# Mixing steps after every sixth projection matmul, and attention in a written order on TensorE and SyncE

## The chip, the core and the metric

The kernel runs on one core of a Trainium2 chip. The metric is the device time of one execution in microseconds (us). TensorE multiplies matrices into PSUM; VectorE, ScalarE and GpSimd work on what comes out; SyncE issues most DMAs. A difference of 0.2% (6 us) is about what a measurement of this kernel can tell from none.

## What is computed

One decoder block on 2048 tokens of width 1024, in float32. Its input projection feeds two groups of heads side by side: eight heads of RWKV-7 time mixing and four heads of differential attention. Output projection, a residual sum and a gated feed-forward part with a short convolution follow. Cut to what the change touches:

```
xn   = rms_norm(x);  proj = xn @ w_in            # 26 column blocks of 128
# time mixing, per token and head:
sa    = state @ (-kk)
state = state * w + sa (kk * a)^T + v k^T
y     = state @ r
# attention, per head h and query block of 128:
s_c  = q_c k_c^T / 8 - slope * distance, causal, c = 0, 1
attn = softmax(s_0) - lam * softmax(s_1)
o    = attn @ v
h    = x + rms_norm(concat(y_rwkv, o) @ w_out);  out = h + feed_forward(h)
```

## The kernel before

**Order of work.** Four stages follow each other: the projection with time mixing woven in, attention, the output projection, the feed-forward part. A planner orders each engine's instructions by readiness in its own time line and by source order. Inside `tc.manual_schedule(engines=...)` the instructions of the named engines keep the order of the source. Before, that holds for TensorE in the projection stage alone.

**Projection.** `Proj.product` makes one block of 128 columns by 512 tokens: 24 matmuls, three for each of eight k (high and low parts of the split operands, L293 to L295). After each three, `Pace.tick` runs every step that is due at that tick. The block is evicted by `shift` (for time mixing) or `evict` (for attention's Q, K, V) and goes to DRAM.

**Time mixing.** `Rwkv.group` is a generator for 128 tokens; there are 16, started `PITCH` = 34 ticks apart, so three are under way at once. Each `yield` names the tick at which the next step is due. The steps with matmuls, in order: z and za (L498, L500), n2 (L515), the turn of its result (L464), the spread (L470), bo (L550), two score steps (L563), V's turn (L582), two turns of keys (L592), wp (L607); then the join of two half inverses, which starts at `JOIN`: xp (L641), a product with bda (L647), one with bdx (L651); then for each of two chunks rp (L666), sp (L672), yp and up (L680 to L688); then mp, vs, a turn, a spread and gp. Between the scores and the join, VectorE runs a chain of 31 pairs of small operations (L612, L614) on data that goes through DRAM (adr, ab), and the result goes through DRAM too (xdr, x1t).

**Attention.** `Attn.steps` walks over 64 units, a head h and a query block qb of 128. `scores` makes, for both maps c, tiles of up to 512 keys in PSUM (L844, L845, and the causal mask L847 on the last); VectorE evicts each with its minimum (L849), ScalarE takes the exponentials (L858), VectorE combines the two maps (L869). `output`, for the unit two back (`LAG` = 2), transposes the weights in blocks of up to four (tp, L887), ScalarE copies them (at, L889), and the value products follow (op, L893). PSUM has four banks for scores, two for transposes, two for outputs. `fetch_k` loads 512 keys and values, `load_q` 256 queries, both from SyncE. After unit 6 `OutFfn.weights` loads w_out and the convolution's tables, splits w_out, and turns the tables on TensorE.

Of the kernel before, what the change touches and what calls it, by code (L numbers as in the profile page):

```python
# [18 lines left out]
P = 128  # L19
# [110 lines left out]
class Pace:  # L130
# [17 lines left out]

    def tick(self):
        self.run(self.now)  # L150
        self.now += 1

# [5 lines left out]
class Proj:  # L158
# [51 lines left out]
    def start(self, first):  # L210

        xs = [self.alloc(0, g) for g in range(2)]
        xt = []
        for t in range(HALF // P):
            if t == W0:
                self.weights(0, 0)
            if t == TB:
                tab = self.tables()
                self.weights(0, 1)
            xt.append(self.norm(t, first))  # L220
            if t < 4:
                for hf in range(2):
                    self.rows(t, hf, xt[t], xs[0])

        def rest():
            for i in range(8):
                t, hf = 4 + i // 2, i % 2
                self.rows(t, hf, xt[t], xs[1])
                yield 1 + 2 * i
        self.pace.add(tab, 6)  # L230
        self.pace.add(rest(), 1)
        for g in range(2):
            for cb in range(2):
                self.product(0, cb, g)
# [51 lines left out]
    def product(self, half, cb, g):  # L286
        nc, cx = self.nc, self.cx
        wh, wl = self.w[half, cb]
        xh, xl = self.x[half, g]
        n = f"{half}_{cb}_{g}"  # L290
        pp = cx.ps.tile([P, GRP], F32, name=f"pp{n}", tag=cx.mm[0], bufs=cx.mm[1])
        for k in range(KB):
            nc.tensor.matmul(pp, wh[:, k, :], xh[:, k, :], start=(k == 0), stop=False)  # L293
            nc.tensor.matmul(pp, wh[:, k, :], xl[:, k, :], start=False, stop=False)  # L294
            nc.tensor.matmul(pp, wl[:, k, :], xh[:, k, :], start=False, stop=(k == KB - 1))  # L295
            if k == KB - 1:
                self.evict(half, cb, g, pp, n)
            self.pace.tick()

# [50 lines left out]
ARB = 3  # L350
PITCH, JOIN = 34, 64
NGRP = S // RG
# [87 lines left out]
class Rwkv:  # L440
# [31 lines left out]
    def group(self, g):  # L472
        tc, nc, cx, T, U = self.env(g)
        tt, stt = nc.vector.tensor_tensor, nc.vector.scalar_tensor_tensor
        v = cx.rv
# [4 lines left out]
        ch = lambda a: a.unsqueeze(2).unsqueeze(3).broadcast_to([P, 4, NC, 64])  # L480
# [11 lines left out]
        nc.sync.dma_start(vv, src[8:12, :, tok].rearrange("b p t -> p b t"))  # L492
        yield 5

# [15 lines left out]
        for q in range(2):  # L510
            nc.vector.tensor_tensor_scan(flat(cum, q), cx.gate, flat(th, q), 0.0, op0=ALU.mult, op1=ALU.add)
        yield 7
        rn = U([P, 4, RG], "n2")
# [20 lines left out]
        nc.vector.tensor_scalar(tha, tha, -0.5, -0.5, op0=ALU.mult, op1=ALU.add)  # L534
        yield 13
        self.turned(rn, sb, cx.rT[0])
        tt(rk, rk, kp, op=ALU.mult)
        tt(rr, pe[:, :, :, 1:65], rr, op=ALU.mult)
        yield 17
        self.spread(rn, cx.rT[0])  # L540
# [55 lines left out]
        tmp = T([P, 8 * 16], "xtmp")  # L596
        for j in range(31):
            if j % 5 == 0:
                yield 34 + 2 * (j // 5)
            if j == 5:  # L600
                kv = T([P, NC, 4, 64], "kv", SB)
                wp = U([P, NC, 4, 64], "wp")
                for c in range(NC):
                    for hb in range(4):
                        for e in range(2):
                            h, ks = 2 * hb + e, slice(64 * (1 - e), 64 * (1 - e) + 64)
# [3 lines left out]
            n, w = j // 4 + 1, 31 - j  # L610
# [47 lines left out]
        both = [(hb, e, 2 * hb + e, slice(64 * e, 64 * e + 64)) for hb in range(4) for e in range(2)]  # L658
        at = JOIN + 7
        yield at  # L660
        for c in range(NC):
# [6 lines left out]
            tt(rsb, rp, rsb, op=ALU.add)  # L668
            yield at + 10 * c + 3
            sp = U([P, 4, 64], f"sp{c}")  # L670
# [3 lines left out]
            for e in range(2):  # L674
                rs = slice(64 * e, 64 * e + 64)
                nc.scalar.copy(sv[e][rs], sp[rs])
            yield at + 10 * c + 6
            yp = U([P, 4, 64], f"yp{c}")
# [11 lines left out]
            tt(yv, yp, yv, op=ALU.add)  # L690
            yield at + 10 * c + 10


        at += 22
        sg = T([P, RG], "sg")
# [10 lines left out]
        sb = self.power(rl, ALU.add, LN_EPS, f"ln{g}")  # L706
        yield at + 9
        self.turned(rl, sb, cx.rT[1])
# [3 lines left out]
        for hb in range(4):  # L712
            nc.scalar.activation(ybv[:, hb], ybv[:, hb], AF.Identity, bias=v["ln_x_b"][:, hb:hb + 1],
                                 scale=v["ln_x_w"][:, hb:hb + 1])
        yield at + 15
        gp = U([P, 4, RG], "gp")
# [57 lines left out]
class Attn:  # L774
# [48 lines left out]
    def scores(self, h, qb):  # L823
# [12 lines left out]
        for c in range(2):  # L836
            e = [self.T([P, EW], "E", f"{n_}{c}{i}", EB) for i in range(ne)]
            mx = self.T([P, 8], "amx", f"{n_}{c}", 6)
            for ch in range(nch):
                n = min(GRP, nk - ch * GRP)  # L840
                sp = self.U([P, GRP], f"sp{n_}{c}{ch}", *cx.mm)
# [35 lines left out]
    def output(self, h, qb):  # L877
# [3 lines left out]
        op = self.U([P, P], f"op{n_}", *cx.rc)  # L881
        for k4 in range(qb // 4 + 1):
            nb = min(4, qb + 1 - 4 * k4)
            tp = self.U([P, 4, P], f"tp{n_}{k4}", *cx.ra)
            for q in range(nb):
                o = (4 * k4 + q) * P
                nc.tensor.transpose(tp[:, q, :], e[o // EW][:, o % EW:o % EW + P], cx.ident)  # L887
            at = self.T([P, 4, P], "at", f"{n_}{k4}", AB)
            nc.scalar.copy(at[:, 0:nb, :], tp[:, 0:nb, :])  # L889
            v = self.heads[h, k4][2]  # L890
            for q in range(nb):
                kb = 4 * k4 + q
                nc.tensor.matmul(op, at[:, q, :], v[:, q, :], start=(kb == 0), stop=(kb == qb))  # L893
        osb = self.T([P, P], "osb", n_, OB)
# [7 lines left out]
        if qb % 4 == 3:  # L902
            self.done.append((h, qb - 3, self.on))
            self.on = []

    def store(self):
# [10 lines left out]
    def steps(self, heads):  # L917

        units = [(h, qb) for h in heads for qb in range(S // P)]
        for i in range(len(units) + LAG):  # L920
            held = len(self.done)
            if i >= LAG:
                self.output(*units[i - LAG])
            if held:
                self.store()
            if i < len(units):
                self.scores(*units[i])
            yield
        self.store()
# [5 lines left out]
class OutFfn:  # L935
# [6 lines left out]
    def weights(self, pool, tmp):  # L942
# [6 lines left out]
        cb = I["conv_b"][0].rearrange("(b p) -> b p", p=P)  # L949
        ctA = load_table(nc, cx, tmp, nc.sync, [cw[0], cw[1]], "cvA")  # L950
        ctB = load_table(nc, cx, tmp, nc.sync, [cw[2], cb], "cvB")
        for kb in range(KB):
            wr = tmp.tile([P, D], F32, name=f"wor{kb}", tag="wor", bufs=5)
            nc.sync.dma_start(wr, w[:, kb, :])
            split_weight(nc, wr, self.wh[:, kb, :], self.wl[:, kb, :])
        ctA, ctB = ctA(), ctB()
        NB2 = 2 * NFB
# [181 lines left out]
def block_kernel(tc, I, out):  # L1139
    nc = tc.nc  # L1140
    cx = Ctx()
    with ExitStack() as st:
# [18 lines left out]
        with pool("pj", "left") as pp:  # L1161
# [4 lines left out]
            with tc.manual_schedule(engines={mybir.EngineType.PE}):  # L1166
# [9 lines left out]
                for at in products:  # L1176
                    if at == (0, NRW - 1, 1):
                        for i in range(NGRP):
                            pace.add(rw.group(i), pace.now + 3 + PITCH * i)
        of = OutFfn(tc, nc, cx, I, out)  # L1180
        with pool("at", "left") as ap:
# [6 lines left out]
            cx.mm, cx.ra, cx.rc = ("mm", 4), ("ra", 2), ("rc", 2)  # L1188
            cx.const = base
            for i, _ in enumerate(at.steps(range(NH))):  # L1190
                if i == ALONE:
                    right.close()
                    with pool("wt", "left") as tp:
                        of.weights(right.enter_context(pool("ww", "right")), tp)
        with pool("fx", "left") as xp, pool("fw", "left") as wp:
# [25 lines left out]
```

## Time and profile before

| | us |
|---|---|
| median of 3 runs | 3181.59 (3180.8 to 3182.9) |
| the profiled execution | 3182.21 |
| its span | 3180.1 |
| TensorE busy in the span | 3013.1 |
| VectorE busy | 1941.0 |
| ScalarE busy | 1167.8 |

The profile is of one execution. A view of the lines gives, for one line of the source and one shape, how often it ran, its mean duration and the idle time of its engine before it. The view of waits names the instruction that waited, what released it, and for how long in total, how often and at most. The timeline lists instructions by start. A view of windows gives busy times and TensorE's granted clock for stretches of the span; the clock has two levels, 1.2 and 2.4 GHz, and 1.00 is the upper one. Matmuls overlap, so a matmul's duration is longer than its distance from the next one's start.

### The profile page before, as it was taken

To read this page: it belongs to the slowest core of one execution; us is meant where nothing else is said; L and a number is where in the kernel's file an instruction comes from. 1 tells how busy PE (TensorE), PEld (TensorE's weight loads), DVE (VectorE), ACT (ScalarE), POOL (GpSimd) and SP (SyncE) were. 2 spreads that over 40 slices of the span, in tenths; PEclk is the share of its full clock that TensorE was granted. 3 is DMA by queue.
4 is the path that set the end of the run, shared out by engine and by line. 5 is a ranking of instruction groups with operands and counts; after the bars stand their busy time and mean duration, and the time that the engine had idled before them with its cause. 6 is when DMAs were issued, how large, how long until landed. Compare 5 with 4: busy or idle time off the path is not lost.

```text
span 3180.1 us, 46505 instructions
## 1 busy us (share of the span) xinstructions
PE 3013.1 (95%) x17411; PEld 2461.9 (77%) x17411; DVE 1941.0 (61%) x4935; ACT 1167.8 (37%) x2292; POOL 376.6 (12%) x545
## 2 busy tenths in 40 slices
PE   7998999999999698899999999999999999999997
PEld 6876777777777487788788888888888788888886
DVE  6366768667774386778455455555557555555556
ACT  5242333333332376677333322222224322222223
POOL 4211112222222112111100000000000000000002
PEclk9998999999999798999999999999999999999999
DMA  8443333444533623331444111111114311111112
GB/s 301 120 145 95 84 94 105 107 106 117 138 102 90 173 64 79 95 79 49 149 150 168 53 40 60 47 47 47 45 55 139 100 53 40 53 50 50 47 34 86
DMA packets 356786, 290.82 MB, mean 91 GB/s; under 512 B 111391, under 2 KB 306562, under 8 KB 356562
## 3 DMA queue, kind: packets, MB, share of 16 engines
q1 hardware_dynamic: 337282, 232.70, 25.5%
q0 software_dynamic: 16976, 50.96, 5.0%
q10 hardware_dynamic: 2304, 4.20, 0.4%
q8 instruction: 138, 2.26, 0.3%
q14 instruction: 86, 0.70, 0.1%
HBM read 208.91 MB, written 78.07 MB: 90 GB/s over the span
## 4 chain that ended last, share of the span: by engine, by line
PE 72%; DVE 11%; DMA 7%; issue 5%; SPq 2%; ACT 2%; POOL 1%; DVEq 0%; POOLq 0%; ACTq 0%
PE fp L103 10%; PE fp L105 10%; PE fp L104 10%; PE dn L104 5%; PE dn L103 5%; PE dn L105 5%; PE pp L293 3%; PE op L893 3%; PE pp L294 3%; PE pp L295 3%; PE po L103 2%; PE po L105 2%; PE po L104 2%; DVE X L614 2%; DVE xtmp L612 2%
## 5 line engine op out<-in xcount | busy, mean ns | idle before, releaser
L1076 DVE TENSOR_TENSOR acc<-dn,acc 128x512 f32<-128x512 f32 x320 | 211.4, 686 | 224.4 <-PE dn L105 222.1
L103 PE MATMUL fp<-f1h,uh 128*128 128x512 f32 x704 | 275.6, 392 | 3.9 <-DVE fcarry L1041 3.9
L104 PE MATMUL fp<-f1l,uh 128*128 128x512 f32 x704 | 275.1, 391 | 0.0
L105 PE MATMUL fp<-f1h,ul 128*128 128x512 f32 x704 | 275.1, 391 | 0.0
L104 PE MATMUL dn<-dl,gh 128*128 128x512 f32 x704 | 274.5, 390 | 0.0
L103 PE MATMUL fp<-f0h,uh 128*128 128x512 f32 x704 | 274.2, 389 | 0.0
L105 PE MATMUL fp<-f0h,ul 128*128 128x512 f32 x704 | 274.1, 389 | 0.0
L104 PE MATMUL fp<-f0l,uh 128*128 128x512 f32 x704 | 274.0, 389 | 0.0
L103 PE MATMUL dn<-dh,gh 128*128 128x512 f32 x704 | 271.8, 390 | 1.9 <-DVE acc L1076 1.9
L105 PE MATMUL dn<-dh,gl 128*128 128x512 f32 x704 | 263.4, 390 | 0.0
L849 DVE TENSOR_SCALAR_CACHE_REDUCE E<-sp 128x512 f32<-128x512 f32 (+3 forms) x320 | 186.5, 606 | 62.8 <-PE sp L845 25.8
L97 DVE TENSOR_TENSOR ul<-ur,uh 128x1024 fp32r<-128x1024 f32 x88 | 107.7, 1225 | 186.6 <-ACT uh L96 186.6
L1037 DVE SCALAR_TENSOR_TENSOR u<-fp,cvA,u 128x511 f32<-128x511 f32 x176 | 131.3, 746 | 119.4 <-ACT u L1035 119.4
L612 DVE TENSOR_TENSOR xtmp<-X,ab 128x60 f32<-128x60 f32 (+24 forms) x496 | 107.1, 216 | 130.4 <-DMA ab<-adr 95.7
L96 ACT CAST dh<-dr 128x1024 fp32r<-128x1024 f32 x44 | 44.4, 1047 | 387.3 <-PE dn L105 383.9
L893 PE MATMUL op<-V,at 128*128 128x128 f32 x1088 | 164.1, 294 | 15.0 <-ACT at L889 14.8
L893 PEld LDWEIGHTS op<-V,at 128*128 128x128 f32 x1088 | 150.7, 206 | 28.7 <-ACT at L889 22.6
L844 PE MATMUL sp<-kab_a,qa 128*128 128x512 f32 (+3 forms) x320 | 140.9, 444 | 26.2 <-DMA qa<-qq 15.9
L858 ACT ACTIVATE E<-E,asc 128x1024 f32<-128x1024 f32 (+7 forms) x160 | 153.4, 964 | 19.6 <-DVE asc L854 19.1
L1035 ACT ACTIVATE u<-fp,cvB 128x512 f32<-128x512 f32 x176 | 136.4, 776 | 59.4 <-PE fp L105 59.2
L103 PEld LDWEIGHTS fp<-f1h,uh 128*128 128x128 f32 x704 | 133.0, 189 | 32.2 <-issue 4.3
L103 PEld LDWEIGHTS dn<-dh,gh 128*128 128x128 f32 x704 | 132.2, 188 | 30.1 <-DVE acc L1076 2.3
(341 smaller groups left out, 6965.9 us busy)
## 6 DMA issues: line engine op xcount, KB each, us to landing
ur<-in_w_up SPq DMA_DIRECT2D x88, 512.0 KB
wr<-in_w_in SPq DMA_DIRECT2D x52, 512.0 KB
dr<-in_w_down SPq DMA_DIRECT2D x44, 512.0 KB
rw<-e POOLq DMA_DIRECT2D x56, 256.0 KB, 2.7
x<-in_x SPq DMA_DIRECT2D x16, 512.0 KB
xn<-x POOLq DMA_DIRECT2D x16, 512.0 KB, 6.6
xr<-xn SPq DMA_DIRECT2D x32, 256.0 KB
ab<-adr SPq DMA_DIRECT2D x64, 128.0 KB
```

What stands on the lines that cost most here:

```text
L97: nc.vector.tensor_tensor(wl, wr, wh.bitcast(F32), op=ALU.subtract)
L103: nc.tensor.matmul(out, lh(kb), rh(kb), start=(kb == 0), stop=False)
L104: nc.tensor.matmul(out, lh(kb), rl(kb), start=False, stop=False)
L105: nc.tensor.matmul(out, ll(kb), rh(kb), start=False, stop=(kb == n - 1))
L612: tt(tv, X[:, 0:n, j:j + 1].broadcast_to([P, n, w]), ab[:, j:j + 1, j + 1:32].broadcast_to([P, n, w]), op=ALU.mult)
L844: nc.tensor.matmul(sp[:, 0:n], qa[:, c, qs], ka[:, c, 0:n], start=True, stop=False)
L849: nc.vector.tensor_scalar(e[ch * GRP // EW][:, eo:eo + n], sp[:, 0:n], -1.0, None, op0=ALU.mult, op1=ALU.min, accum_out=mx[:, ch:ch + 1])
L858: nc.scalar.activation(e[i][:, 0:n], e[i][:, 0:n], AF.Exp, bias=nm, scale=-1.0, accum_out=z)
L893: nc.tensor.matmul(op, at[:, q, :], v[:, q, :], start=(kb == 0), stop=(kb == qb))
L1035: nc.scalar.activation(u, pp, AF.Identity, bias=wb(b), scale=w2(b))
L1037: stt(u[:, 1:GRP], pp[:, 0:GRP - 1], w1(b), u[:, 1:GRP], op0=ALU.mult, op1=ALU.add)
L1076: nc.vector.tensor_tensor(acc[:, t, ds_], po, acc[:, t, ds_], op=ALU.add)
```

## The change

`Pace.ticks(2)` takes the place of `tick`: due steps run after every six projection matmuls, and those of two ticks together. Offsets become even, `JOIN` goes from 64 to 62, the groups start three ticks sooner, the steps of the two chunks stand four ticks apart instead of three or four, and the tail (vs, turn, spread, gp) is spaced anew.

In attention TensorE and SyncE keep the source's order. `scores` and `output` become generators that take turns: up to four score tiles, then two blocks of transposes with their copies, then the next score tiles, then the value products of those two blocks and the next two blocks of transposes, until both are done. `output` of the unit two back came before `scores` in the source; now its first part stands behind the first four score tiles. The convolution tables lie in another pool, and their transposes come four units after the loads.

```diff
-    def tick(self):
-        self.run(self.now)
-        self.now += 1
+    def ticks(self, n):
+        self.run(self.now + n - 1)
+        self.now += n
...
-            self.pace.tick()
+            if k % 2:
+                self.pace.ticks(2)
...
-PITCH, JOIN = 34, 64
+PITCH, JOIN = 34, 62
...
-        yield 5
+        yield 6
...
-        yield 7
+        yield 8
...
-        yield 13
+        yield 14
...
-        yield 17
+        yield 18
...
-        at = JOIN + 7
+        at = JOIN + 6
...
-            yield at + 10 * c + 3
+            yield at + 12 * c + 4
...
-            yield at + 10 * c + 6
+            yield at + 12 * c + 8
...
-            yield at + 10 * c + 10
-
-
-        at += 22
+            yield at + 12 * c + 12
+
+
+        at += 24
...
-        yield at + 9
+        yield at + 10
...
-        yield at + 15
+        yield at + 16
...
+                if c * nch + ch and (c * nch + ch) % 4 == 0:
+                    yield
...
-        for k4 in range(qb // 4 + 1):
-            nb = min(4, qb + 1 - 4 * k4)
-            tp = self.U([P, 4, P], f"tp{n_}{k4}", *cx.ra)
-            for q in range(nb):
-                o = (4 * k4 + q) * P
-                nc.tensor.transpose(tp[:, q, :], e[o // EW][:, o % EW:o % EW + P], cx.ident)
-            at = self.T([P, 4, P], "at", f"{n_}{k4}", AB)
-            nc.scalar.copy(at[:, 0:nb, :], tp[:, 0:nb, :])
-            v = self.heads[h, k4][2]
-            for q in range(nb):
-                kb = 4 * k4 + q
-                nc.tensor.matmul(op, at[:, q, :], v[:, q, :], start=(kb == 0), stop=(kb == qb))
+        todo = list(range(qb // 4 + 1))
+        ats = []
+        for pair in [todo[i:i + 2] for i in range(0, len(todo), 2)] + [[]]:
+            self.sums(op, qb, h, ats)
+            ats = []
+            for k4 in pair:
+                nb = min(4, qb + 1 - 4 * k4)
+                tp = self.U([P, 4, P], f"tp{n_}{k4}", *cx.ra)
+                for q in range(nb):
+                    o = (4 * k4 + q) * P
+                    nc.tensor.transpose(tp[:, q, :], e[o // EW][:, o % EW:o % EW + P], cx.ident)
+                at = self.T([P, 4, P], "at", f"{n_}{k4}", AB)
+                nc.scalar.copy(at[:, 0:nb, :], tp[:, 0:nb, :])
+                ats.append((k4, nb, at))
+            if pair:
+                yield
...
+    def sums(self, op, qb, h, ats):
+        for k4, nb, at in ats:
+            v = self.heads[h, k4][2]
+            for q in range(nb):
+                kb = 4 * k4 + q
+                self.nc.tensor.matmul(op, at[:, q, :], v[:, q, :], start=(kb == 0), stop=(kb == qb))
...
+            parts = [self.scores(*units[i])] if i < len(units) else []
             if i >= LAG:
-                self.output(*units[i - LAG])
+                parts.append(self.output(*units[i - LAG]))
+            while parts:
+                parts = [p for p in parts if next(p, parts) is not parts]
             if held:
                 self.store()
-            if i < len(units):
-                self.scores(*units[i])
...
-        ctA, ctB = ctA(), ctB()
+        def tables():
+            self.tables(ctA(), ctB())
+        return tables
...
-                            pace.add(rw.group(i), pace.now + 3 + PITCH * i)
+                            pace.add(rw.group(i), pace.now + PITCH * i)
...
+            region = tc.manual_schedule(engines={mybir.EngineType.PE, mybir.EngineType.SP})
+            region.__enter__()
             for i, _ in enumerate(at.steps(range(NH))):
                 if i == ALONE:
                     right.close()
                     with pool("wt", "left") as tp:
-                        of.weights(right.enter_context(pool("ww", "right")), tp)
+                        tables = of.weights(right.enter_context(pool("ww", "right")), tp)
+                if i == ALONE + 4:
+                    tables()
+            region.__exit__(None, None, None)
```

## Rows read from the trace of the kernel before

**Rows 1.** Busy us (and instructions) of five engines, granted clock, DMA, by stage.
```profile
145.00:1062.00 917.00, 859.35 (x7077) 672.01 (x7076) 603.42 (x1811) 316.79 (x629) 202.20 (x259) 0.97 0.40 107
1062.00:1526.00 464.00, 393.88 (x2546) 337.54 (x2545) 329.18 (x1171) 311.74 (x782) 82.35 (x135) 0.89 0.35 93
```

**Rows 2.** The same view, stretches of attention: TensorE, its loads, VectorE, ScalarE, GpSimd.
```profile
1062.00:1120.00 58.00, 27.80 (x99) 20.82 (x98) 25.97 (x82) 22.19 (x51) 8.08 (x14) 0.53 0.82 209
1190.00:1420.00 230.00, 203.06 (x1334) 176.06 (x1333) 165.34 (x603) 157.34 (x407) 41.45 (x67) 0.92 0.35 87
1250.00:1300.00 50.00, 49.28 (x357) 43.78 (x357) 42.96 (x152) 40.50 (x100) 10.08 (x14) 1.00 0.21 59
1500.00:1526.00 26.00, 19.43 (x124) 16.62 (x123) 12.48 (x28) 15.02 (x31) 4.15 (x7) 0.87 0.33 96
```

**Rows 3.** TensorE's waits in attention: us in total, times, longest.
```profile
PE vp L809 <- DMA vtl<-vT: 17.0, 1, 17.0
PE sp L844 <- DMA qa<-qq: 15.9, 5, 4.3
PE op L893 <- ACT at L889: 14.8, 24, 3.4
```

**Rows 4.** SyncE's waits from 1030 to 1120 us, the longest.
```profile
SPq L43 <- DVE cvB_st L41: 21.9, 1, 21.9
```

**Rows 5.** SyncE's timeline at the start of attention: start, us, DMA issued.
```profile
1068.36 0.94 SPq L792 DMA_DIRECT2D vtl<-vT  x1
```

**Rows 6.** TensorE's waits in the projection stage, 145 to 1062 us.
```profile
PE xp L641 <- DMA x1t<-xdr: 10.6, 1, 10.6
PE rp L666 <- DVE X L614: 8.9, 6, 2.7
...
PE up L683 <- ACT sav L676: 6.2, 8, 1.0
PE sp L672 <- issue: 3.7, 4, 2.6
```

**Rows 7.** TensorE's timeline in the projection stage, two places with a spread (L470).
```profile
477.69 0.66 PE L470 MATMUL vs<-rT,sel 40*128 40x128 f32 x4
478.28 0.50 PE L293 MATMUL pp<-x3h,wh 128*128 128x512 f32 x1
...
496.72 0.66 PE L470 MATMUL n<-rT,sel 40*128 40x128 f32 x4
497.31 0.50 PE L293 MATMUL pp<-x3h,wh 128*128 128x512 f32 x1
```

**Rows 8.** SyncE's timeline, the load of x1t in one group.
```profile
460.95 0.33 SPq L619 DMA_DIRECT2D x1t<-xdr  x1
```

**Rows 9.** TensorE's timeline, the transposes that read it.
```profile
464.03 0.43 PE L641 MATMUL xp<-ident,x1t 32*128 32x32 f32 x4
```

**Rows 10.** VectorE's lines in attention by shape: count, busy us, mean ns, idle before.
```profile
L849 DVE TENSOR_SCALAR_CACHE_REDUCE E<-sp 128x512 f32<-128x512 f32 x224 | 150.2, 686 | 49.2 <-PE sp L845 25.8 <-PE tp L887 19.4 <-PE sp L847 2.8
...
L97 DVE TENSOR_TENSOR wol<-wor,woh 128x1024 fp32r<-128x1024 f32 x8 | 9.7, 1223 | 12.9 <-ACT woh L96 12.9
...
L869 DVE SCALAR_TENSOR_TENSOR E<-E,asc,E 128x768 f32<-128x768 f32 x8 | 8.1, 1015 | 0.1
```

**Rows 11.** TensorE's timeline in large units: transposes (L887), value products (L893), scores (L844).
```profile
1480.04 1.11 PE L893 MATMUL op<-V,at 128*128 128x128 f32 x8
1480.91 0.48 PE L844 MATMUL sp<-kab_a,qa 128*128 128x512 f32 x1
...
1484.60 1.04 PE L887 MATMUL tp<-ident,E 128*128 128x128 f32 x8
1485.87 1.16 PE L893 MATMUL op<-V,at 128*128 128x128 f32 x8 [0.24 <-ACT at L889]
...
1507.86 1.83 PE L893 MATMUL op<-V,at 128*128 128x128 f32 x14 [1.29 <-ACT at L889]
```

**Rows 12.** ScalarE's lines in attention by shape, the widest exponential.
```profile
L858 ACT ACTIVATE E<-E,asc 128x1024 f32<-128x1024 f32 x80 | 91.8, 1148 | 8.9 <-DVE asc L854 8.3 <-DVE asc L863 0.4
```

More of the change, by code (lines that the diff above doesn't have):

```diff
@@ L229, in rest @@
                 yield 1 + 2 * i
-        self.pace.add(tab, 6)
+        self.pace.add(tab, 4)
         self.pace.add(rest(), 1)
@@ L949, in weights @@
         cb = I["conv_b"][0].rearrange("(b p) -> b p", p=P)
-        ctA = load_table(nc, cx, tmp, nc.sync, [cw[0], cw[1]], "cvA")
-        ctB = load_table(nc, cx, tmp, nc.sync, [cw[2], cb], "cvB")
+        ctA = load_table(nc, cx, pool, nc.sync, [cw[0], cw[1]], "cvA")
+        ctB = load_table(nc, cx, pool, nc.sync, [cw[2], cb], "cvB")
         for kb in range(KB):
@@ L955, in weights, with tables @@
             split_weight(nc, wr, self.wh[:, kb, :], self.wl[:, kb, :])
-        ctA, ctB = ctA(), ctB()
+        def tables():
+            self.tables(ctA(), ctB())
+        return tables
+    def tables(self, ctA, ctB):
         NB2 = 2 * NFB
```

## The prediction

> **What bounds the kernel now.** I read the busy time by stage first. In the projection stage (145 to 1062 us) TensorE is busy 859 of 917 us, in the attention stage (1062 to 1526) 394 of 464, with granted clocks of 0.97 and 0.89 [rows 1]. VectorE follows with 603 and 329. So TensorE bounds both, and a change of order can only win back what TensorE loses there: idle time, and half of what it does at 1.2 GHz instead of 2.4.
>
> For attention I sum that loss window by window. A granted clock c over a width w means 2(1-c)w at the lower level; TensorE's work in that time costs double. From 1062 to 1120 it idles 30 us and does nearly all its 27.8 us at the lower clock: 30 + 13 = 43 lost. From 1190 to 1420, where heads 1, 2 and 3 begin, it idles 27 and some 33 of its busy 203 us are at the lower clock: 27 + 16 = 43. From 1500 to 1526, 6.6 + 2.5 = 9 [rows 2]. What remains of the stage loses 8 by the same count. So 103 of 464 us are lost, and the work at full clock is 361. Between heads hardly anything is lost: 1250 to 1300 has 49.3 of 50 us busy [rows 2].
>
> Then the waits, to see what each loss is. The first score of the stage stands behind the load of V (17.0 us); loads of Q cost 15.9 more; the value products wait 14.8 for ScalarE's copies of the transposed weights [rows 3]. The 17.0 us have a cause in SyncE's order: SyncE stood 21.9 us at the conv table's load, which waited for a memset of its tile, and V's load came behind it and behind four loads of w_out, at 1068.36 [rows 4, 5]. The planner had put these ahead of head 0.
>
> In the projection the waits that belong to mixing are smaller: 10.6 us once, at the first group's xp; 8.9 at the state products rp behind the one releaser that the row names, 17 with the others; 6.2 at up; 3.7 at sp, 7.2 with the others [rows 6].
>
> **The change, part by part, in the projection.** No instruction is added or removed; steps that were due at 34 ticks a group are due at 17 double ticks. Writing out the offsets modulo 34, 25 steps with matmuls fall into 19 gaps between projection matmuls before and into 15 after. What is a gap worth? The spread (four matmuls) takes 0.59 us from its first matmul to the next projection matmul both alone (496.72 to 497.31) and behind z in a shared gap (477.69 to 478.28) [rows 7]. So the price sits on the steps, not on the gap; four gaps fewer in each of 16 periods are worth 0 to 0.05 us each, 0 to 3 us. I take 1. The Trainium skill (TensorE: Matmul & The Clock Gate, Part 2) says that back-to-back matmuls hide the array's drain and an isolated one cannot; at its some 175 ns for each of 64 gaps the saving would be 11 us instead of 1 (estimate from that page); the row is against it.
>
> The waits: sp to yp goes from 3 ticks to 4, so the 6.2 us at up go, and so do some 2 of the 7.2 at sp. For rp of the second chunk the distance from yp stays 4 ticks, but n2 now stands between them, and 0.9 us of 1.1 in each of about 12 groups is covered: -8 us. Against it stands the join: its offset from the score steps is 38 ticks before and 36 after, some 2.9 us at 1.47 us per tick (917 us over 624 ticks). In the group at 464 us the load of x1t was issued at 460.95 and its transpose began at 464.03 [rows 8, 9]; the first group shows 2.2 us from issue to use, so 0.9 us was spare there. In 5 of the 16 groups the spare time is under 2 us, in the others up to 15. A stall in one group gives the next its time back, so I count 2 to 3 us in half of such groups and at the first: +11, bounds 4 and 25. Sum: -1 - 8 - 8 + 11 = about -6, bounds -18 and +12; since a faster mixing eats into the same slack I take -4.
>
> **Attention, the start.** Head 0's loads now come before w_out's in SyncE's order. What is queued behind: w_out's eight loads and the tables' four stand ahead of Q's group 4 and K's chunk 2, both for unit 8, and three of the eight wait for a split to free a buffer. VectorE's eight splits, 1.22 us each [rows 10], lie today in a stretch where it is busy 26 of 58 us [rows 2]; after, beside units 6 to 10, where it is short: +10. The first three units have nothing beside them, and from a first score to its transposes go a score tile, its eviction, two exps, the small steps and the combination, some 4.2 us, of which 1.5 are scores: +3. So 43 becomes 13. Bounds: 5, if the splits fit, and 43, if V's load stays gated by memory that the last products hold.
>
> **Attention, the steps.** Q and K for a new head now have two large units of lead, so I give the loads nothing at the three later head starts. What takes their place is order. In each step the last transposes are followed at once by their value products, with no scores left to put between. Eight transposes and then a product cost 0.24 us of idle today [rows 11], four cost 0.44 more, since the first copy is then the last one. Over the 16 steps of a head (two have none, two have a second one) these add to 7 us. Beside large scores the copy can stand behind an exp: then it is 1.29 [rows 11], and an exp of 1024 is 1.15 [rows 12]. For the six large steps of a head I take 0.85 each, 5 us. In the small units VectorE sets the pace instead: unit 5 needs two evictions of 512 columns (0.69 each), two of 256, a combination of 1.02 [rows 10] and some 2 us of small steps with the two narrow evictions, 4.4 us less overlap, where TensorE needs 2.9 (eight value products are 0.87 [rows 11]). Summed over units 2 to 11 VectorE lacks about 8 us a head, of which four PSUM banks carry 2.5; the small units' waits lie inside this. So a head loses 5 + 5.5 + 1.5 (its first two steps, whose outputs are large) + 3 (lower clock while TensorE idles a quarter) = 15, four heads 60, against 43 + 8 = 51 now. Bounds a head: 7, the waits alone at their least, to 24, with 1.3 at every step and the clock halved.
>
> The end: 9 now, and 11 after, with four waits in the last two outputs. Sum: 13 + 60 + 11 = 84 lost instead of 103: -19 us. The tables' transposes four units later cost nothing: 0.2 us of TensorE, and their reader is the feed-forward stage.
>
> Total, against the profiled execution (3182.2; the median of the runs shown is 3181.6): 3182 - 4 - 19 = 3159 us.
>
> **The rivals.**
> 1. The start's gain is had and the steps cost no more than now (51 instead of 60), since the planner still orders VectorE and ScalarE around TensorE's fixed order, and the join's slack holds: -19 - 9 - 10 = 3182 - 38 = 3144, with the best bounds 3120. For it: 1250 to 1300 is nearly full today. Against: that stretch got there with an order free to move scores in front of a wait.
> 2. Slower: a step's last value products stand behind ScalarE's two exps, not one. Place: the ten larger steps of each head. Price: two exps of 1.15 and the copy instead of 0.85 is 1.6 more, for 40 steps 64 us; 3159 + 64 = 3223. It decides from 23/40 = 0.6 us per step more than I took. For it: ScalarE is busy 312 of 464 us [rows 1], and exps stand ahead of copies in the source. Against: these waits sum to 14.8 now [rows 3].
> 3. No change: V's first load stays where it is, for memory or for the writes of K just before it, so that the start saves 10 instead of 30: 3159 + 20 = 3179.
> 4. The clock: at each head start TensorE is busy in short pieces, and runs of transposes stand among them. If units 2 to 7 (15 us of work) all run at 1.2 GHz, that is up to 9 us a head beyond VectorE's pace: 3159 + 36 - 12 already counted = 3183 and, with the waits of large steps, up to 3195. For it: 0.53 at the start [rows 2]. Against: 1250 to 1300 is granted 1.00 with transposes throughout [rows 2]. The Trainium skill (TensorE: Matmul & The Clock Gate, Part 4) says that the full clock does not engage for transposes; by that rule it would be this case, and that last row does not agree.
>
> **How the numbers follow.** A measurement tells 0.2% (6 us) from no change, so "same" is 3175 to 3188. Forecast 3159 (own range 3144 to 3175): 0.46. Rival 1 (3115 to 3144): 0.16. Rival 3: 0.12. Rival 2 (3188 to 3235): 0.18. Rival 4: 0.08, half of it slower. So faster 0.62, same 0.16, slower 0.22. A range of 3122 to 3206 leaves out about 0.04 below and 0.13 above.
>
> **What would show it.** Right: V's and Q's first loads ahead of w_out's; the first score within 5 us of the last projection matmul; no loads among TensorE's waits at head starts; waits for the copies at the value products 40 to 60 us in all instead of 14.8; idle at units 2 to 11 put down to VectorE; up's waits gone and xp's longer. Wrong: the copies' waits over 100 us (rival 2); the granted clock under 0.89 in the stage (rival 4); the first score still at 1083; a projection stage that moves by over 15 us, which I argue only from slack.

## The result, and the profile after

The change makes the kernel slower: 3199.41 us (median; 3196.88 to 3201.48) against 3181.59 (3177.29 to 3186.54). The ratio is 1.0054, 95% interval 1.0043 to 1.0065. The forecast was 3159, faster: the time lies inside the stated range of 3122 to 3206, but on the other side of the kernel before.

To place the 17.5 us between the two profiled spans (3180.1 and 3197.6) I cut TensorE's records at the first z, the last projection matmul and the first matmul of the output projection. I cut them again where the granted clock changes: what TensorE does at the lower level counts half as work and half as loss. Idle is the time in which no matmul runs.

| | length | work at full clock | idle | lost to the lower clock |
|---|---|---|---|---|
| projection, before | 880.0 | 807.2 | 54.7 | 18.1 |
| projection, after | 892.3 | 801.0 | 59.5 | 31.8 |
| attention, before | 458.0 | 355.6 | 70.1 | 32.2 |
| attention, after | 464.3 | 362.5 | 80.7 | 21.1 |

The rest differs by -1. So projection gives +12.3 and attention +6.3, where -4 and -19 were forecast. These are single executions, and those of one kernel differ with the clock: 18 of the kernel before lie between 3175.0 us (granted clock 0.975) and 3195.8 (0.970), so several us of a clock column can be chance. The view of windows (width, then busy us of TensorE, its loads, VectorE, ScalarE, GpSimd, then clock) of the kernel after, by the stretches of [rows 1], then the start of attention and what follows it:

```profile
145.00:1062.00 917.00, 854.71 (x7023) 669.87 (x7023) 605.39 (x1807) 314.13 (x624) 200.66 (x257) 0.96 0.40 106
1062.00:1526.00 464.00, 387.88 (x2525) 326.17 (x2524) 328.63 (x1167) 310.69 (x771) 92.88 (x133) 0.95 0.32 91
...
1074.00:1132.00 58.00, 46.95 (x240) 37.83 (x238) 43.72 (x153) 40.15 (x99) 16.47 (x21) 0.74 0.69 202
1132.00:1539.00 407.00, 337.38 (x2293) 286.20 (x2294) 283.66 (x1014) 273.48 (x681) 76.24 (x113) 0.98 0.26 73
```

The first 58 us of attention have 11 us idle and a clock of 0.74, against 30 and 0.53 in [rows 2]: the start was gained in part. The other 407 have 70 us idle. The tiles in the waits below: rp, sp, xp and up are mixing's products, vp turns V, sp in attention holds scores, tp the transposed weights, op the value products, ot the turned output. TensorE's waits after, first in the projection stage (to hold against [rows 6]), then in attention (against [rows 3]); us in total, times, longest:

```profile
PE xp L642 <- DMA x1t<-xdr: 19.7, 8, 11.1
PE rp L667 <- DVE xtmp L613: 11.1, 5, 3.3
...
PE rp L667 <- DVE X L615: 7.1, 3, 3.3
PE rp L667 <- DVE state L687: 6.9, 4, 3.4
...
PE op L918 <- ACT at L897: 66.3, 76, 2.9
PE ot L926 <- POOL on L907: 4.2, 5, 2.1
PE sp L848 <- DMA kab_b<-kk: 3.5, 1, 3.5
```

The waits at up and sp are gone. Those at rp rose from 17.2 to 26.5 us, all releasers together, and those at xp from one to eight. In attention the loads of V and Q are gone, and the products' waits for ScalarE's copies went from 14.8 to 66.3 us.

One wait at rp shows two things. VectorE's timeline of the kernel after (start, us, line, operation), from shortly before up ends on TensorE (643.4) on:

```profile
642.77 1.27 DVE L512 TENSOR_TENSOR_SCAN t_d<-sgate,t_b 128x256 f32<-128x256 f32 x2
...
644.09 0.68 DVE L720 TENSOR_TENSOR ybv<-ybv,gp 128x512 f32<-128x512 f32 x1
...
645.86 0.69 DVE L528 TENSOR_TENSOR kr<-kr,t_c 128x512 f32<-128x512 f32 x1 [0.20 <-issue]
...
648.36 0.41 DVE L686 TENSOR_TENSOR st<-state,up 128x256 f32<-128x256 f32 x1
648.69 1.38 DVE L532 TENSOR_TENSOR BK<-kr,t_d 64x512 f32<-64x512 f32 x2
...
650.65 0.41 DVE L687 TENSOR_TENSOR state<-st,pc 128x256 f32<-128x256 f32 x1
```

The state update (st, then state) stands behind the scans, gp's product, n2's operations and BK of two other groups, some 7 us of VectorE without a pause worth naming. rp starts at 651.12 after 3.40 us idle. What the clock makes of that, in windows of the kernel after that end with the wait, cover it, follow it, and come after that:

```profile
640.00:647.70 7.70, 7.70 (x81) 6.17 (x80) 7.22 (x23) 5.45 (x13) 2.90 (x4) 1.00 0.29 86
647.70:651.10 3.40, 0.02 (x1) 0.00 (x0) 3.36 (x11) 1.37 (x2) 0.35 (x1) 0.93 0.00 1
651.10:657.40 6.30, 6.28 (x29) 4.74 (x29) 5.01 (x18) 0.00 (x0) 3.62 (x5) 0.50 0.65 172
657.40:667.00 9.60, 9.60 (x95) 7.10 (x94) 7.02 (x20) 1.32 (x3) 2.02 (x2) 1.00 0.26 80
```

The granted clock is 0.50, that is 1.2 GHz, over the 6.3 us after the wait. Half of that, 3.1 us, is lost on top of the 3.4: this wait costs nearly double its length.

### The profile page after: what moved, and what is told of

It reads as the page before. It is cut to its first block, busy times and chain, and to the rows that moved or that the text cites. A ratio compares the mean times of both kernels' runs of the same rounds, so it can differ in the third digit from the quotient of the medians.

```text
span 3197.6 us, 46427 instructions
## 1 busy us (share of the span) xinstructions
PE 3015.6 (94%) x17411; PEld 2459.4 (77%) x17411; DVE 1946.6 (61%) x4935; ACT 1172.5 (37%) x2292; POOL 388.2 (12%) x545
## 4 chain that ended last, share of the span: by engine, by line
PE 71%; DVE 11%; issue 6%; ACT 4%; DMA 4%; POOL 1%; SPq 1%; DVEq 0%; POOLq 0%; ACTq 0%
PE fp L103 10%; PE fp L105 10%; PE fp L104 10%; PE dn L104 5%; PE dn L103 5%; PE dn L105 5%; PE pp L293 4%; PE pp L294 3%; PE pp L295 3%; PE op L918 3%; ACT E L861 2%; PE po L103 2%; PE po L105 2%; PE po L104 2%; DVE E L852 1%
## 5 line engine op out<-in xcount | busy, mean ns | idle before, releaser
L918 PE MATMUL op<-V,at 128*128 128x128 f32 x1088 | 154.7, 292 | 66.3 <-ACT at L897 66.3
L918 PEld LDWEIGHTS op<-V,at 128*128 128x128 f32 x1088 | 135.9, 199 | 84.0 <-ACT at L897 83.9
L105 PEld LDWEIGHTS fp<-f1h,ul 128*128 128x128 f32 x704 | 132.7, 189 | 28.0
```

Source lines behind the costliest of these rows:

```text
L105: nc.tensor.matmul(out, ll(kb), rh(kb), start=False, stop=(kb == n - 1))
L918: self.nc.tensor.matmul(op, at[:, q, :], v[:, q, :], start=(kb == 0), stop=(kb == qb))
```

## The experiments

The planner orders VectorE and ScalarE anew for each kernel. So two kernels with the same source in one stage can still differ there, and the same attention took 464 us in the change and 483 alone. In these two TensorE's list from the first vp on is the same instruction for instruction, and VectorE's differs in 260 places of 2946. Stage lengths are those of one profiled execution; times are medians, and ratios are against before, run beside each kernel. In brackets, work, idle and clock are the three columns of the table above.

### The two parts, each alone

e1: the diff above `Attn` and the groups' new starts, with attention as before.

> Mixing's new ticks and offsets alone, attention as before. Theory A, the two parts of the change add: by the stages of the two traces the projection stage ends 12 us later and the rest stays, so 3194 us (ratio 1.003 to 1.005), with some 27 us of waits at rp and some 20 at xp. Theory B, the projection stage ends late only because SyncE or the memory layout of attention changed with it: within 3 us of before. The prediction on record had -4 us for this part.

Measured: 3187.4 us, ratio 1.0011 (1.0001 to 1.0020). The projection stage took 895.5 us (work 800.5, idle 56.7, clock 38.3), the waits are those of after (rp 27.1, xp 19.7). That is theory A's stage, but the total is only +3 us, which by itself is theory B's. In the profiled execution attention took 445.8 instead of 458.0, by less time at the lower clock (17.1 lost instead of 32.2). The planner's order differs there (TensorE's list in 384 places of 2530); whether the order or the clock of that execution made it was not isolated. e9 and e10 below settle the cost of the mixing where attention is written out.

e2: the diff from `Attn` on without the groups' starts, mixing as before.

> Attention in the source's order alone, mixing as before. Theory A, the parts add: the attention stage takes 464 us instead of 458, so 3187 us (ratio 1.001 to 1.003); value products wait some 66 us for the copies, the first score stands directly behind the last projection matmul. Theory B, the late end of mixing is what spoils attention: some 3160 to 3170 us, as in the prediction's -19.

Measured: 3207.1 us, 1.0069 (1.0052 to 1.0086). Mixing 883.8, attention 483.1 (work 362.2, idle 91.3, clock 29.6). The cost is in attention, and 20 us larger than theory A had it:

```profile
PE op L917 <- ACT at L896: 73.7, 76, 2.9
```

Theory B fell: this attention is slow behind the old mixing too.

### Mixing: ticks or offsets

e3, on before (as in the change, the start of the step `tab` moves along, from tick 6 to 4, and to 2 in e14):

```diff
...
-            self.pace.tick()
+            if k % 2:
+                self.pace.ticks(2)
```

> Steps run after every six matmuls, but all offsets, JOIN and the starts are those of before; attention as before. Theory A, the new spacing costs the time (at rp VectorE's list holds another group's n2 and z work ahead of the state update; the join comes earlier): within 4 us of before, rp's waits about 17 us. Theory B, the grouping costs it (steps that stood in two gaps now queue together on VectorE and TensorE waits in one place): 8 to 14 us slower, rp's waits 25 us or more.

e4, on e1:

```diff
-            if k % 2:
-                self.pace.ticks(2)
+            self.pace.ticks(1)
```

> The new offsets, JOIN and starts, but due steps run after every three matmuls as before; attention as before. Theory A (the spacing costs it): 8 to 14 us slower, rp 25 us and xp 20 us of waits. Theory B (the grouping costs it): within 4 us of before.

Measured: e3 3165.8 us, 0.9944 (0.9930 to 0.9957); e4 3190.6, 1.0023 (1.0012 to 1.0033). The projection stage takes 880.8 us in e3 (work 799.9, idle 52.7, clock 28.2) and 903.6 in e4 (800.7, 58.3, 44.6). Theory A holds for the stage: with the new offsets it is 12 to 24 us longer whichever way the ticks run, with the old ones it is not. By time e4 is only 6 us slower, short of theory A's 8 to 14, and its waits are not the expected 25 and 20: rp has 16.4 us, xp more.

```profile
PE xp L641 <- DMA x1t<-xdr: 27.5, 9, 10.4
```

The two together make 27.8 us before, 30.9 in e3, 43.9 in e4 and 46.8 in e1, so the sum goes with the offsets, and the ticks decide how it is shared out. In e4 all offsets and starts are even, so its steps meet in nearly the same gaps as with double ticks; the work says so. I did not expect e3 to be faster. Its profile puts the gain in attention (446.9 us), where the planner's order is another one; its other executions reach 9 us below the profiled one, and where those 9 lie no profile shows. Behind the same written attention, e10 against e5 below, the stages put the gain in the projection.

Both kernels do some 7 us less work than before. I counted, in TensorE's order, the places where another tile's matmul follows one of the projection: 325 before, 260 after and in e1, 257 in e3, 268 in e4. In the kernel after that is 6.2 us less for 65 gaps, 0.10 us each.

e14, on e3, goes on: steps after every twelve matmuls, 150 gaps.

```diff
-            if k % 2:
-                self.pace.ticks(2)
+            if k % 4 == 3:
+                self.pace.ticks(4)
```

> The offsets of before, attention as before, and due steps run after every twelve matmuls. The gaps between projection matmuls fall from 325 before (257 with double ticks) to 150. Theory A, each gap costs 0.10 us of TensorE whatever stands in it: its work at full clock in the stage is 807 - 17 = 790 us, and with the waits of double ticks the time is 3150 to 3158. Theory B, the saving with double ticks was another thing (the clock, fewer steps alone), and steps in lumps make VectorE late: work stays near 800, waits grow by 10 us or more, 3170 to 3190.

Measured: 3165.8 us, 0.9951 (0.9933 to 0.9969). Work 781.1, that is 26 us less than before for 175 gaps. Some of it has only moved: nine projection matmuls now run before the first z, and eight of gp behind the last projection matmul. Counted from the start of the kernel it is 22.6 us, 0.13 each: theory A's price, and a little more. The time that A gave was missed by 8 us: idle 64.6 and clock 40.4 make 105 us against 73 before, and the stage takes 886.1. Waits grew by 10 us as theory B had it, but its time, 3170 to 3190, was missed too. The saving came back as waits (sp 16.7 us, xp 20.3) and lower clock. Where the price of a gap stands can be seen in the timeline of any of them; after:

```profile
551.83 0.39 PE L295 MATMUL pp<-x4h,wl 128*128 128x512 f32 x1
552.15 0.68 PE L673 MATMUL sp<-kv,M 64*64 64x64 f32 x16
552.76 0.50 PE L293 MATMUL pp<-x3h,wh 128*128 128x512 f32 x1
553.10 0.39 PE L294 MATMUL pp<-x3l,wh 128*128 128x512 f32 x1
553.33 0.40 PE L295 MATMUL pp<-x3h,wl 128*128 128x512 f32 x1
```

Projection matmuls start 0.23 us apart (553.10 to 553.33). Into the gap it is 0.32 (551.83 to 552.15), and behind it 0.34 (552.76 to 553.10): 0.09 and 0.11 more. Not every step has the first part: ahead of zw the distance is 0.24 (475.58 to 475.82, before).

### What rp and xp wait for

e7, on e1, moves the second chunk's rp and all behind it by two ticks:

```diff
...
-            yield at + 12 * c + 12
+            yield at + 14 * c + (12 if c else 14)
...
-        at += 24
+        at += 26
```

> Mixing's new ticks and offsets alone, with the second chunk's rp two ticks (six projection matmuls) later and all that follows it too. Theory A, rp waits because the state update of the first chunk stands in VectorE's list behind another group's n2 and z work and the distance of four ticks does not cover it: rp's waits fall from 27 us to under 12, the half-clock stretches behind them go too, and the time falls by 8 to 15 us against mixing alone (3172 to 3180 us). Theory B, rp waits for whatever VectorE has in its list and a later rp only meets other work there: rp's waits stay above 20 us and the time within 4 us of mixing alone (3184 to 3192).

e8, on e1:

```diff
-PITCH, JOIN = 34, 62
+PITCH, JOIN = 34, 66
```

> Mixing's new ticks and offsets alone, with the join four ticks later (66 instead of 62, that is two ticks behind that of before). Theory A, the eight short waits at xp come from the join's two ticks earlier: they go, xp's waits fall from 20 us to the first group's 11, and the time falls by 5 to 12 us (3175 to 3183). Theory B, those waits are given back by the next group (a stall in one shortens the next), or the later join moves the state products to places where they wait more: the time within 4 us of mixing alone (3184 to 3192).

e13, on e1:

```diff
-        yield 8
+        yield 12
         rn = U([P, 4, RG], "n2")
```

> Mixing's new ticks and offsets alone, with another group's n2 step at 12 ticks instead of 8, so that it is no longer due at the tick of yp and up. Theory A, n2's VectorE work stands ahead of the state update and makes rp late: rp's waits fall from 27 us to under 15, and the time by 6 to 12 us against mixing alone (3175 to 3182). Theory B, the planner puts other work there or the wait moves to xp as when rp stood later: the sum of waits at rp, sp and xp stays at 42 to 50 us and the time within 4 us of mixing alone (3184 to 3192).

Measured: e7 3200.2 us, 1.0046 (1.0028 to 1.0064); e8 3176.1, 0.9972 (0.9961 to 0.9984); e13 3189.8, 1.0016 (1.0005 to 1.0027). The waits that tell them apart, the first line from e7, the next two from e8, the others from e13:

```profile
PE xp L642 <- DMA x1t<-xdr: 38.7, 11, 10.6
```

```profile
PE xp L642 <- DMA x1t<-xdr: 20.7, 5, 8.0
...
PE rp L667 <- DVE state L687: 6.9, 5, 3.3
```

```profile
PE rp L667 <- DVE state L687: 14.6, 8, 3.4
PE rp L667 <- DVE xtmp L613: 12.6, 5, 3.6
PE xp L642 <- DMA x1t<-xdr: 12.5, 4, 8.5
PE n L465 <- POOL rs_kk L459: 11.1, 7, 4.5
```

In e7 the waits at rp are 0.1 us instead of 27.1, as theory A had it, but xp's doubled to 38.7, and the stage is 893.6 us, as long as without the edit. (e7's time is outside both theories' ranges; its profile has the difference to e1 in attention, 461.6.) In e13 rp waits as long as in e1 (28.1 us), xp 7 us less and n2's turn 11 us more: n2's place is not what makes rp late. In e8 theory A's time came, with a stage of 888.4, but for another reason: xp waits as long as before the edit, only in five places, and rp fell to 8.1. Of the 7 us that the stage is shorter than in e1, 6 are work (794.5 with 273 gaps, 13 more than e1). So the number of gaps does not set the work alone; which steps stand next to each other differs too, and its price was not isolated. So theory A fell in e13, and half of it in e7 and e8. What holds: all three move waits from one place to another, and over the variants on e1 the stage's idle time stays between 52 and 62 us. VectorE is busy some 590 us of the stage in each. That a chain through VectorE sets this floor fits the timeline above but is not shown; what sets its length stays open.

### Attention: who stands in front of the copies

e5, on e2: the output of the unit two back takes its turn first, so that each block's products stand behind four score tiles.

```diff
-            parts = [self.scores(*units[i])] if i < len(units) else []
-            if i >= LAG:
-                parts.append(self.output(*units[i - LAG]))
+            parts = [self.output(*units[i - LAG])] if i >= LAG else []
+            if i < len(units):
+                parts.append(self.scores(*units[i]))
```

> Attention alone as in the previous run of it, but in each step the output of the unit two back takes its turn first: two blocks of transposes, four score tiles, the value products of those blocks and two more of transposes, four score tiles, value products. No product of a step then stands directly behind its own transposes. Theory A, the loss of attention is the last pair's products behind copies that ScalarE takes after two exponentials: waits for the copies fall from some 70 us to 15 to 25, and the time from 3207 to 3150 to 3165 us (ratio 0.990 to 0.995). Theory B, any fixed order on TensorE costs it, since scores can no longer move in front of a wait: waits move to the scores and the time stays at 3190 or more.

e11, on e2:

```diff
...
-                nc.scalar.activation(e[i][:, 0:n], e[i][:, 0:n], AF.Exp, bias=nm, scale=-1.0, accum_out=z)
+                nc.scalar.activation(e[i][:, 0:P], e[i][:, 0:P], AF.Exp, scale=-1e-3, accum_out=z)
```

> Attention alone as the change has it, but each exponential covers 128 columns only, without its bias, and the mask's fill is smaller; so most of the softmax is left out, and ScalarE is nearly free for the copies. The orders of the written engines are the same. Theory A, the products wait for copies that stand behind exponentials: waits for the copies fall from 74 us to 77 waits of the bare copy, 25 to 38 us, none over 1 us. Theory B, they wait for the copy itself or for the eviction of the weights behind VectorE: 60 us or more stay.

Measured: e5 3143.5 us, 0.9868 (0.9850 to 0.9886); e11 3137.2 in one execution. The waits for the copies, e5 first, then e11:

```profile
PE tp L894 <- DVE E L871: 14.4, 19, 1.8
PE ot L925 <- POOL on L906: 11.2, 5, 6.1
PE op L917 <- ACT at L896: 10.2, 23, 1.6
```

```profile
PE op L917 <- ACT at L896: 30.6, 64, 1.0
```

Theory A holds in both, against B, and e5 is 7 us below its range. With short exps (most of the softmax is left out) there remain 64 waits of the bare copy, 0.48 us each. With the transposes first 10 us are left, and attention takes 412.6 us (work 356.7, idle 48.2, clock 7.7) instead of 483.1: of the 70 us, 43 are idle time, 22 lower clock and 6 work. Of the 64 us that the copies' waits lost a part moved to the combination of the maps on VectorE (tp) and to GpSimd (ot). One wait of the kernel after shows what happened there, TensorE first, then ScalarE:

```profile
1256.70 0.49 PE L895 MATMUL tp<-ident,E 128*128 128x128 f32 x3
1259.93 0.94 PE L918 MATMUL op<-V,at 128*128 128x128 f32 x6 [2.74 <-ACT at L897]
```

```profile
1255.52 1.15 ACT L861 ACTIVATE E<-E,asc 128x1024 f32<-128x1024 f32 x1 [2.79 <-DVE asc L857]
...
1256.67 0.81 ACT L861 ACTIVATE E<-E,asc 128x640 f32<-128x640 f32 x1
...
1257.48 1.13 ACT L861 ACTIVATE E<-E,asc 128x1024 f32<-128x1024 f32 x1
...
1258.61 0.81 ACT L861 ACTIVATE E<-E,asc 128x640 f32<-128x640 f32 x1
...
1259.42 0.45 ACT L897 COPY at<-tp 128x384 f32<-128x384 f32 x1
```

The copy of the last transposes stands behind four exps, both maps of the newer unit; the first has ended when the transposes begin, three are in the way. ScalarE had been idle 2.79 us before them, waiting for VectorE's minimum. Counted over the kernel after, 30 of the 76 waits have one to three exps between the transposes and the copy; they make 44 of the 66 us.

### SyncE's order

e6, on e2:

```diff
-            region = tc.manual_schedule(engines={mybir.EngineType.PE, mybir.EngineType.SP})
+            region = tc.manual_schedule(engines={mybir.EngineType.PE})
```

> Attention alone with the written order on TensorE, while SyncE's order is the planner's again. Theory A, the early start of attention comes from SyncE's order: V's first load goes back behind w_out's and the first score stands some 15 to 20 us behind the last projection matmul again, the copies' waits stay at some 70 us: 3215 to 3230 us. Theory B, it comes from TensorE's order or from the tables' other pool: the first score stays within 5 us of the last projection matmul and the time is 3200 to 3212.

Measured: 3234.8 us, 1.0156 (1.0130 to 1.0181), 28 more than e2. Theory A, and 5 us above its range:

```profile
PE op L917 <- ACT at L896: 78.3, 74, 7.5
PE vp L809 <- DMA vtl<-vT: 17.8, 1, 17.8
PE sp L846 <- DMA qa<-qq: 8.7, 1, 8.7
```

V's first load is back behind w_out's, and its wait is back as in [rows 3]. So the gain at the start needs SyncE's written order; whether it also needs the tables' other pool, which e6 keeps, was not tested.

### Put together

e9 is the whole change with the edit of e5; e10 is e3 and e5; e12 is e10 with the first group's join, and what counts from it, eight ticks later; e15 is e14 and e5. The edit of e12:

```diff
-        yield JOIN
+        join = JOIN + (8 if g == 0 else 0)
+        yield join
...
```

> The whole change with one edit: in each step the output of the unit two back takes its turn ahead of the scores. Theory A, the change lost on this one order: attention costs some 413 us instead of 464 as in the run of it alone, mixing stays at 892 to 896, so 3146 to 3160 us (ratio 0.988 to 0.992). Theory B, mixing's late end and this attention disturb each other: 3165 us or more.

> Double ticks with the offsets of before, and attention with the transposes first. Theory A, the parts add: 3143 for attention and -18 for mixing give 3122 to 3132 us (ratio 0.980 to 0.984). Theory B, double ticks gained only by a luckier clock at the start of attention (the profiled mixing stage took as long as before), which the new attention has already: 3140 to 3146.

> As the run with the offsets of before and the transposes first, with the first group's join and state products alone eight ticks later. Theory A, the first group's wait at xp (11 us, and the half-clock stretch of 17 us behind it) is a distance too short for a chain that nothing of another group delays: both go, 8 to 15 us less than that run. Theory B, the wait moves to the second group, whose products come closer behind: within 4 us of it.

> The same with the attention that has the transposes first. Theory A: 10 us under the run with double ticks, 3118 to 3124 us. Theory B: 3135 to 3150.

| | us | ratio, interval | projection stage | attention |
|---|---|---|---|---|
| e9 | 3151.0 | 0.9883 (0.9870 to 0.9897) | 895.6 | 412.0 |
| e10 | 3131.8 | 0.9823 (0.9807 to 0.9839) | 876.8 | 410.4 |
| e12 | 3129.9 | 0.9819 (0.9803 to 0.9835) | 879.8 | 411.5 |
| e15 | 3142.7 | 0.9872 (0.9852 to 0.9893) | 882.3 | 413.2 |

e9 and e10 went as theory A has it, e12 and e15 as theory B. One change of turns takes some 50 us off the change and makes it faster than before. e9 and e10 differ in mixing's offsets alone, and attention takes the same in both: the new offsets cost 19 us, by time (3151.0 against 3131.8) and by the projection stage (895.6 against 876.8; 13 of it lower clock, 5 idle, 1 work). e5 and e10 differ in double ticks with the old offsets alone: these take 11 us off the projection stage (888.0 in e5), 7 of them work. So of mixing's two edits the double ticks gain and the offsets lose more. In e12 the second group's xp waits 10.0 us and the first's 3.3, where in e10 the first's waits 11.2. e10 and e12 are some 55 us faster than before.

## Why the prediction was wrong, step by step

Three steps failed. In attention, a step's last value products were priced as standing behind one exp, and stood behind up to three. In the projection, n2 was to cover the wait at rp, which grew instead. And the lower clock that goes with waits was left out at the start of attention and in the projection.

**Attention, -19 forecast, +6.3 measured.** By the forecast's own parts: the start lost 24 us instead of 13, the steps and the end 78 instead of 71, and work, held constant, rose by 7. That is the whole 25.
- The start: the mechanism was right (e6), V's load is issued at 1060.6 and the first score at 1074.50, 0.6 us after the last projection matmul began. The size was 43 to 24 instead of 43 to 13: 11 us are idle, 6 of them in waits for copies, and a clock of 0.74 over 58 us is 30 us at the lower level, some 25 of them busy, half of that lost. I had left nothing at the lower clock.
- The steps: here the mechanism failed. I had 0.44 us for a wait of the bare copy, and e11 measures 0.48. For the copy behind an exp I took 0.85 us in 24 steps, 20 us. It was 30 waits and 44 us, since not one exp but up to three stand in front. Rival 2 named this place and put two exps there (1.6 us more a step; the longest wait has 2.9), but its sign, over 100 us of such waits, did not come: 66 us, where I had expected 40 to 60. I gave it 0.18 because these waits were small in [rows 3], but there the planner could move scores in front of a wait, and the change takes just that away; with other work put between, they fall to 10 us (e5). Lower clock outside the start cost 9 us where I had 12.
- No loads wait at the later head starts: right. The idle at units 2 to 11 put down to VectorE: wrong, only 3 us of TensorE's waits in the stage name it, most others name ScalarE's copies. Behind these VectorE can still stand, as the 2.79 us above show; how much of the 66 us is its was not measured.
- Work at full clock, which I held constant, rose by 7 us in after and e2 and by 1 in e5, which issues the same matmuls. Each wait breaks TensorE's stream, and a break has a price (below); that this is the whole of the 7 us was not shown.

**Projection, -4 forecast, +12.3 measured.**
- Gaps: -1 forecast, -6.2 measured for 65 gaps. [rows 7] time the spread from its first matmul to the next projection matmul, and the price stands outside that: at the second place 0.09 us ahead of the first (496.40 to 496.72) and 0.11 behind the next (497.31 to 497.65). The estimate of 11 us from the Trainium skill (TensorE: Matmul & The Clock Gate, Part 2), which I dismissed on that row, was about as far off above as I was below.
- Waits at up and sp: -8 forecast, -13 measured. Right in kind.
- rp: -8 forecast, +9 measured. The step "n2 now stands between them", by which it was to cover the wait, failed. What rp waits for stands in VectorE's list, which I had not read, and not on TensorE. Making TensorE arrive later brought nothing in e7 and e13, where the waits moved; e8 gained, mostly in work.
- xp: +11 forecast, +9 measured. Right: 11.1 us in the first group, and 0.4 to 2.6 in seven others.
- The clock: not in the sum, +14 measured. I counted a wait at its length. In the records of the stage TensorE falls to the lower clock seven times before and twelve times after; of these, three come during or right behind a wait at rp or xp before, nine after. e9 and e10 point the same way: their medians lie 19 us apart, with 13 us of lower clock between the two profiles.
- These add to -6 - 13 + 9 + 9 + 14 = +13, against 12.3.

**Rivals and signs.** Rival 4 looked for the clock in attention, where it rose from 0.89 to 0.95 with the start's stall gone; it fell in the projection stage. The Trainium skill's rule there (TensorE: Matmul & The Clock Gate, Part 4: no full clock for transposes) did not decide this stage after either: 0.98 over 407 us with transposes in every step, among scores and value products. No run here shows a stretch of transposes alone. Rival 1's gain, -28 from attention (-19 and -9), is less than what e5 and e9 get with one order changed (-46 by the stages, 458.0 to some 412), so a written order can gain and this one did not. A stage "that moves by over 15 us, which I argue only from slack" was named as what would make the prediction wrong; it moved by 12, and lies 16 from the forecast.

## What to carry to other kernels

Before you write out one engine's order, look at what each of its instructions will wait for on the engines that stay planned: put between a producer and its consumer enough work to cover the whole queue in front of the copy, not the copy alone. Price a wait with the clock that follows it in the trace. When a wait vanishes in an experiment, look at the stage's idle sum before calling it gained. Where a planner rearranges the stage that was left alone, compare two kernels whose other stage is written out, as e9 and e10.

## What was not expected of the hardware

- A wait of 3.4 us at rp was followed by 6.3 us at a clock of 0.50, and the projection stage lost 32 us to the lower clock after, 18 before, with only 5 us more idle.
- A break in TensorE's stream of projection matmuls cost some 0.10 us (65 gaps fewer) to 0.13 us (175 fewer), with no idle shown: it is in the distances of the starts around it, 0.32 and 0.34 us instead of 0.23. It is no fixed price: e8 has 13 gaps more than e1 and 6 us less work.
